# The squares of a decoder's first RMS norm, summed by TensorE alone, with its input loaded from two DMA queues

## The chip, the cores and the metric

The kernel runs on one core of a Trainium2 chip. The metric is the device time of one execution in microseconds (us). The core has five engines with instruction queues of their own: PE (TensorE: matrix products and transposes, with its weight loads listed as PEld), DVE (VectorE), ACT (ScalarE), POOL (GpSimd) and SP (SyncE, which issues DMAs here). Each engine works through its queue in order. An instruction whose input isn't ready holds up what is behind it on its own engine, and nothing else.

## The reference: what is computed

One inference step of a two-layer decoder, for a prompt of 512 tokens behind 16 meta tokens and for 8 sequences of 8 new tokens: 592 tokens of width 1024. Each layer is a gated feed-forward block, a mixer (a state-space scan and stick-breaking attention side by side, with a paged cache of keys and values for the new tokens) and a second feed-forward block, each behind an RMS norm. The change touches only the first norm, ahead of the first product:

```
def rms_norm(x, g):
    xf = x.astype(jnp.float32)
    y = xf * lax.rsqrt(jnp.mean(xf * xf, axis=-1, keepdims=True) + EPS)
    return (y * g.astype(jnp.float32)).astype(x.dtype)

def swiglu(h, w_gu, w_down):
    g, u = jnp.split(h @ w_gu, 2, axis=-1)
    return (jax.nn.silu(g) * u) @ w_down

x = x + 0.5 * swiglu(rms_norm(x, lp['norm_ffn1']), lp['ffn1_w_gu'], lp['ffn1_w_down'])
```

## The kernel before

All 592 tokens are processed at once, with the features on the partitions: x is eight tiles of 128 features by 592 tokens (`X[0]` to `X[7]`, k = 0 to 7). Products are kept close to float32 precision by splitting each operand into a high and a low part of a faster type and adding three products, high by high, high by low and low by high (`mm3`, L605, 128x128 by 128x296, two halves of the tokens). The weights come in blocks of 512 x 256 (`raw`, L586, three buffers) and are split half a block at a time: ACT makes the high part `whi` (L595), DVE the low part `wlo` (L596). A norm isn't applied ahead of its product: the product is made with the unscaled x times the gain, and its result is multiplied by R, the reciprocal root of each token's mean square, when it is evicted from PSUM (`times_r`, L231).

The first norm is built in `load_x`, called by `setup`. x is loaded from memory token by token, in six pieces (meta tokens, four blocks of 128 prompt tokens, 64 new tokens) and two halves of the features, all from SP's queue (L399), the first weight block between the halves. For each k, PE transposes the six pieces into two PSUM tiles `xps` (L406), DVE copies the first (L407) and ACT the second (L408) into `X[k]`. `norm_tile` then makes four things from `X[k]`: `xh`, the high part of x times the gain (L446, ACT); `xl`, the low part (L447, DVE); and the square `sq`, on GpSimd for even k (L451) or ACT for odd k (L453). The squares of k = 1 to 6 are added into that of k = 0 (L459), by GpSimd for k = 1, 3, 5 and by DVE for k = 2, 4, 6. `norm_end` hands the two remaining tiles to `factor`, a generator that runs a step with each product: it waits 8 steps, sums both tiles over the partitions with 10 one-column products on PE (L476, five groups of 128 tokens, two tiles), takes the reciprocal root on DVE (L522 to L529, some 14 instructions on five columns, one behind the other), waits 20 steps, spreads the result over the partitions with 10 products on PE (L208) and copies R from PSUM with ACT (L573). In the profile, a product on plain float32 operands such as L476 has two records. Until R is there (`hold`) the finished column blocks of the first product stay in PSUM; three fit, and the fourth has to wait for the first eviction.

The order of the instructions on each engine isn't written by hand. A scheduler places them by priority and by its own estimate of when each could run. In the mixers the program adds two small tables (`PRI` and `UNIT`) that set priorities of work that is to fill PE's gaps. An instruction that is placed elsewhere in the first norm can therefore change the order in a mixer 450 us later, though no line of it has changed. The feed-forward blocks have one chain of products, and leave the scheduler little to choose.

## Time and profile before

| | us |
|---|---|
| median of 3 runs | 2719.44 (2717.28 to 2721.03) |
| profiled execution, its own time | 2716.29 |
| its span in the trace | 2714.5 |
| PE busy | 2611.9 |
| DVE, ACT, GpSimd busy | 1505.0, 981.8, 315.6 |
| first norm, start to steady products | 50 |
| mixer 1, mixer 2 (first sum of the norm ahead to first sum of the norm behind) | 479.88, 483.83 |

All numbers of one row of a profile come from one execution. A row of the timeline gives the start, the time to the end of the last of its instructions, the engine, the line, the operation, output and inputs with their shapes, and how often it is repeated; in brackets stands the idle time of that engine ahead of it, and what ended it. A row of the waits says who waited for whom: total us, times, longest. In a row of the windows the busy time of each engine in one stretch is followed by the clock that TensorE was granted (1.00 is full speed), the share of the DMA engines' time in use, and the rate. A matrix instruction is recorded longer than it keeps the next from starting, so the spacing of starts is the price of one.

### The profile page before, as it was taken

The page shows a single profiled execution, that of the slowest core. Times are in us where ns is not written, and L with a number is a line of the kernel's source. Part 1 is how long each engine was busy: PE and PEld are TensorE (multiplying, and loading weights), DVE is VectorE, ACT ScalarE, POOL GpSimd, SP SyncE. Part 2 cuts the span into 40 slices and gives each one's busy share as a digit, 9 for nine tenths or more (in the row PEclk, how much of TensorE's full clock was granted, in tenths as well). Part 3 has the DMA queues.
Part 4 walks back from the last instruction along what each step waited for, and adds up shares of the span by engine and source line. Part 5 has one row for each costly group of instructions (what it writes and reads, how often), then busy time and mean ns, then how long its engine had stood idle before and what let it go on. Part 6 is the DMA issues. An engine that isn't in the chain of part 4 may idle for free.

```text
span 2714.5 us, 51301 instructions
## 1 busy us (share of the span) xinstructions
PE 2611.9 (96%) x21547; PEld 2469.2 (91%) x21547; DVE 1505.0 (55%) x3005; ACT 981.8 (36%) x1773; POOL 315.6 (12%) x288
## 2 busy tenths in 40 slices
PE   8999999999878999999999999999997899999999
PEld 7999999888656999999999999998875579999999
DVE  5444345477886744444554343454777867434444
ACT  3323224255654332222332222233556544323222
POOL 1000000024443100000000000000334431000000
PEclk9999999999998999999999999999998989999999
DMA  3232234347776122222222323254577762222222
GB/s 111 79 116 86 79 109 130 125 142 262 269 267 230 55 78 86 86 78 78 78 78 79 101 85 94 74 157 125 183 248 247 256 219 71 78 86 86 78 87 81
DMA packets 245111, 343.28 MB, mean 126 GB/s; under 512 B 32808, under 2 KB 196720, under 8 KB 244880
## 3 DMA queue, kind: packets, MB, share of 16 engines
q1 hardware_dynamic: 208016, 205.77, 24.5%
q0 software_dynamic: 36864, 134.23, 14.5%
q8 instruction: 169, 2.77, 0.4%
q14 instruction: 62, 0.51, 0.1%
HBM read 320.29 MB, written 19.66 MB: 125 GB/s over the span
## 4 chain that ended last, share of the span: by engine, by line
PE 60%; DVE 6%; DMA 3%; ACT 2%; issue 1%; POOL 0%; SPq 0%; DVEq 0%; ACTq 0%; POOLq 0%
PE g L605 53%; DVE kt L1493 2%; DMA v<-in_cache_v,vi 1%; PE v L926 1%; DMA kn<-in_cache_k,ki 1%; PE po L208 1%; PE po L211 1%; DVE st L1298 1%; DVE x L799 0%; PE pw L476 0%; PE z L211 0%; PE sc L211 0%; DVE pst L1298 0%; PE zt L1350 0%; PE pw L1534 0%
## 5 line engine op out<-in xcount | busy, mean ns | idle before, releaser
L605 PE MATMUL g<-xl,whi 128*128 128x296 f32 (+1 forms) x3392 | 1016.9, 300 | 1.7 <-DVE xl L447 1.7
L605 PE MATMUL g<-xh,wlo 128*128 128x296 f32 (+1 forms) x3392 | 1012.5, 299 | 3.4 <-DVE wlo L596 3.4
L605 PE MATMUL g<-xh,whi 128*128 128x296 f32 (+1 forms) x3392 | 1013.8, 300 | 1.6 <-DVE gs L231 1.2
L595 ACT ACTIVATE whi<-raw 128x512 fp32r<-128x512 f32 (+1 forms) x664 | 412.7, 622 | 1363.5 <-PE g L605 1280.4
L596 DVE TENSOR_TENSOR wlo<-raw,whi 128x512 fp32r<-128x512 f32 (+1 forms) x664 | 450.7, 679 | 598.0 <-ACT whi L595 541.1
L605 PEld LDWEIGHTS g<-xh,wlo 128*128 128x128 f32 x3392 | 640.2, 189 | 5.4 <-DVE wlo L596 4.1
L605 PEld LDWEIGHTS g<-xh,whi 128*128 128x128 f32 x3392 | 639.6, 189 | 6.0 <-issue 2.6
L605 PEld LDWEIGHTS g<-xl,whi 128*128 128x128 f32 x3392 | 640.6, 189 | 4.8 <-DVE xl L447 2.8
L605 PE MATMUL g<-hl,whi 128*128 128x296 f32 (+1 forms) x1408 | 417.9, 297 | 0.0
L605 PE MATMUL g<-hh,wlo 128*128 128x296 f32 (+1 forms) x1408 | 417.7, 298 | 0.0
L605 PE MATMUL g<-hh,whi 128*128 128x296 f32 (+1 forms) x1408 | 416.8, 298 | 0.0
L1487 POOL DMA_INDIRECT kn<-in_cache_k,ki x128 | 137.0, 1070 | 1554.6 <-PE g L605 931.5
L605 PEld LDWEIGHTS g<-hl,whi 128*128 128x128 f32 x1408 | 265.2, 188 | 0.0
L605 PEld LDWEIGHTS g<-hh,wlo 128*128 128x128 f32 x1408 | 264.3, 188 | 0.0
L605 PEld LDWEIGHTS g<-hh,whi 128*128 128x128 f32 x1408 | 263.9, 188 | 0.0
L1493 DVE STREAM_TRANSPOSE kt<-kn 128x512 f32<-128x512 f32 x256 | 163.4, 680 | 41.8 <-PE sc L211 21.7
L1552 POOL DMA_INDIRECT v<-in_cache_v,vi x128 | 144.2, 1127 | 280.6 <-DVE kt L1493 128.0
L704 DVE SCALAR_TENSOR_TENSOR x<-g,x 128x296 f32<-128x296 f32 (+1 forms) x192 | 88.2, 464 | 119.1 <-PE g L605 118.5
L231 DVE TENSOR_TENSOR us<-g,R 128x296 f32<-128x296 f32 (+1 forms) x176 | 81.6, 464 | 129.5 <-PE g L605 129.4
L231 DVE TENSOR_TENSOR gs<-g,R 128x296 f32<-128x296 f32 (+1 forms) x176 | 80.7, 464 | 123.1 <-PE g L605 121.4
L691 ACT ACTIVATE hh<-us 128x592 fp32r<-128x592 f32 (+1 forms) x88 | 61.2, 696 | 62.4 <-DVE us L689 62.4
L605 PE MATMUL g<-mh,whi 128*128 128x296 f32 (+1 forms) x256 | 78.0, 305 | 2.0 <-DVE ot L231 2.0
(372 smaller groups left out, 2894.5 us busy)
## 6 DMA issues: line engine op xcount, KB each, us to landing
raw<-in_ffn_w_gu SPq DMA_DIRECT2D x176, 512.0 KB
raw<-in_ffn_w_down SPq DMA_DIRECT2D x80, 512.0 KB
raw<-in_w_in SPq DMA_DIRECT2D x44, 512.0 KB
raw<-in_w_out SPq DMA_DIRECT2D x16, 512.0 KB
spill<-x SPq DMA_DIRECT2D x16, 296.0 KB
x<-spill SPq DMA_DIRECT2D x16, 296.0 KB
raw<-in_ffn_w_down SPq DMA_DIRECT2D x16, 256.0 KB
xt<-in_x_prompt SPq DMA_DIRECT2D x8, 256.0 KB
```

Source lines behind the costliest of these rows:

```text
L208: i = self.nc.tensor.matmul(*a, **k).ins
L211: i = self.nc.tensor.matmul(*a, **k).ins
L231: self.nc.vector.tensor_tensor(tv[0:P, h, :], ps[h][0:P, 0:self.n], rv[0:P, h, :], ALU.mult)
L595: nc.scalar.activation(hi[:, 0:nk], s, AF.Copy)
L596: nc.vector.tensor_tensor(lo[:, 0:nk], s, hi[:, 0:nk].bitcast(F32), ALU.subtract)
L605: mm = nc.tensor.matmul(ps[h][:, 0:self.n], w[:, k, :], self.hv(x)[:, h, :], start=(first and k == 0 and i == 0), stop=(last and k == nk - ...
L691: nc.scalar.activation(hh[:, a:b], u[:, a:b], AF.Copy)
L704: nc.vector.scalar_tensor_tensor(v, p, 0.5, v, ALU.mult, ALU.add)
L926: nc.tensor.matmul(ps[c], x[:, t0:t0 + 128], w.rearrange("p x c -> p (x c)"), start=(k == 0 and i == 0), stop=(k == 7 and i == 2))
L1487: nc.gpsimd.indirect_dma_start(kn, None, self.kflat, bass.IndirectOffsetOnAxis(ap=self.kidx[l][:, s, i:i + 1], axis=0))
L1493: nc.vector.transpose(kt[:, 2 * u:2 * u + 2].rearrange("p t h i -> p t (h i)"), kns[u][:, :, 256 * quad:256 * quad + 256])
L1552: nc.gpsimd.indirect_dma_start(v.rearrange("p k c -> p (k c)"), None, self.vflat, bass.IndirectOffsetOnAxis(ap=self.vidx[l][:, i, e:e + 1] ...
```

## The change

Four edits go together. All eight squares are made by ACT. None is added to another: for each k, PE sums the square at once with five one-column products that accumulate over k in one PSUM tile `B0`, 40 products in place of 10. `factor` then starts from these sums, without a wait of 8 steps. And every second piece of x (the first and third block of the prompt, and the new tokens) is issued from ACT's DMA queue; the meta tokens and the other two blocks stay on SP's.

```
         for h in range(2):
-            for (t, n, _), (s, _, _) in zip(toks, src):
-                nc.sync.dma_start(t[0:n, 512 * h:512 * h + 512], s[:, 512 * h:512 * h + 512])
+            for i, ((t, n, _), (s, _, _)) in enumerate(zip(toks, src)):
+                (nc.scalar if i % 2 else nc.sync).dma_start(t[0:n, 512 * h:512 * h + 512], s[:, 512 * h:512 * h + 512])
             if h == 0:
                 self.raw0 = self.raw(I["ffn1_w_gu"][0], 0, 4, 0, 256)
+        self.B0 = self.own("pw", [128, 128])
         for k in range(KD):
...
             if k == 0:
                 self.split0 = self.split(self.raw0, 4, 0)
-            self.norm_tile(k, "norm_ffn1", 0, nc.gpsimd if k in (1, 3, 5) else nc.vector,
-                           None if k % 2 else nc.gpsimd)
+            self.norm_tile(k, "norm_ffn1", 0, own=True)
+
+            for i, t0 in enumerate(self.groups()):
+                nc.tensor.matmul(self.B0[:, i:i + 1], self.sq[:, t0:t0 + 128], self.c_ones, start=(k == 0 and i == 0),
+                                 stop=(k == KD - 1), skip_group_check=True)
...
-    def norm_tile(self, k, nm, l, eng=None, sqeng=None):
+    def norm_tile(self, k, nm, l, eng=None, own=False):
...
         sq = self.tmp("sq")
-        if sqeng:
-            sqeng.tensor_tensor(sq[:, a:b], x[:, a:b], x[:, a:b], ALU.mult)
-        else:
-            nc.scalar.activation(sq[:, a:b], x[:, a:b], AF.Square)
-        if k == 0:
+        nc.scalar.activation(sq[:, a:b], x[:, a:b], AF.Square)
+        if own:
+            self.sq = sq
+        elif k == 0:
             self.acc = sq
...
-    def factor(self, squares, inv, wait):
+    def factor(self, squares, inv, wait, made=None):
...
-            A, B = self.own("po", [128, 512]), self.own("pw", [128, 128])
+            A, B = self.own("po", [128, 512]), made or self.own("pw", [128, 128])
...
     def norm_end(self):
-        self.factor([self.acc, self.sq], 1.0 / D, (8, 0, 20))
-        self.acc = self.sq = None
+        if self.B0:
+            self.factor([], 1.0 / D, (0, 0, 20), self.B0)
+        else:
+            self.factor([self.acc, self.sq], 1.0 / D, (8, 0, 20))
+        self.acc = self.sq = self.B0 = None
```

Lines of the changed kernel have moved by up to six: L605 is L611 there, L447 is L451, and the new sums are L415. Where the instructions now stand is shown at three places. The first is PE in the first norm, where the transposes of the second half of x begin (`xps`, the number tells one PSUM tile from the next). Before:

```order
L406 MATMUL xps_187<-call,xt 128x64
L406 MATMUL xps_203<-call,xt 128x16
L406 MATMUL xps_220<-call,xt 128x16
L406 MATMUL xps_237<-call,xt 128x16
L406 MATMUL xps_203<-call,xt 128x128
L406 MATMUL xps_220<-call,xt 128x128
L406 MATMUL xps_237<-call,xt 128x128
```

With the change, the same place, down to the first product of the feed-forward block (`g`):

```order
L407 MATMUL xps_263<-call,xt 128x128
L415 MATMUL pw<-call,sq 128x1 x10
L407 MATMUL xps_221<-call,xt 128x128 x2
L407 MATMUL xps_242<-call,xt 128x128 x2
L415 MATMUL pw<-call,sq 128x1 x10
L407 MATMUL xps_222<-call,xt 128x128
L407 MATMUL xps_222<-call,xt 128x64
L407 MATMUL xps_284<-call,xt 128x16
L407 MATMUL xps_284<-call,xt 128x128 x3
L611 MATMUL g_307<-xh,whi 128x296
```

The sums of the first four squares stand behind 30 and 34 of the 48 transposes, so that 20 sums, beside 46 transposes, now precede the first product. The other 20 sums follow after 18 products, with 31 products between them and the spread of R; before, the 10 sums came after 102 products.

The second place is ACT's queue from the start of the kernel. Before:

```order
L408 ACT_TABLE_LOAD
L408 ACTIVATE x_104<-xps_133 128x192
L408 ACTIVATE x_105<-xps_153 128x192
L408 ACTIVATE x_106<-xps_170 128x192
L446 ACTIVATE xh<-x_104,par 128x592
L453 ACTIVATE sq<-x_105 128x592
L595 ACTIVATE whi<-raw 128x512
```

With the change:

```order
L399 DMA xt<-in_x_prompt 128x512 x2
L399 DMA xt<-in_x_sample 64x512
L399 DMA xt<-in_x_prompt 128x512 x2
L399 DMA xt<-in_x_sample 64x512
L409 ACT_TABLE_LOAD
L409 ACTIVATE x_104<-xps_134 128x192
L450 ACTIVATE xh<-x_104,par 128x592
L454 ACTIVATE sq<-x_104 128x592
L454 ACTIVATE sq<-x_105 128x592
L601 ACTIVATE whi<-raw 128x512
L454 ACTIVATE sq<-x_106 128x592
```

Six DMA issues now precede the table load, and a square more stands ahead of the first `whi`. The last four issues each wait for an earlier transfer that used the same semaphore, the last two for blocks of the first half of x.

The third place is PE near the end of mixer 1, where the products with the gathered values (`po<-v,wt`) end and the output projection (`g<-mh,whi`) goes on. Before:

```order
L208 MATMUL po<-v,wt 32x256
L211 MATMUL po<-v,wt 32x256 x7
L208 MATMUL z_9608<-wp,vk 64x16
L211 MATMUL z_9608<-wp,vk 64x16 x15
L211 MATMUL z_9608<-w_9633,vk 64x16 x4
L208 MATMUL po<-v,wt 32x256
L211 MATMUL po<-v,wt 32x256 x7
L208 MATMUL po<-v,wt 32x256
L211 MATMUL po<-v,wt 32x256 x7
L208 MATMUL po<-v,wt 32x256
L211 MATMUL po<-v,wt 32x256 x7
L605 MATMUL g_9852<-mh,whi 128x296
```

With the change:

```order
L208 MATMUL po<-v,wt 32x256
L211 MATMUL po<-v,wt 32x256 x7
L208 MATMUL z_9583<-wp,vk 64x16
L211 MATMUL z_9583<-wp,vk 64x16 x15
L211 MATMUL z_9583<-w_9608,vk 64x16 x4
L1381 LDWEIGHTS mall
L1381 MATMUL z_9632<-mall 128x32
L1575 MATMUL po<-call,ob 128x16 x2
L611 MATMUL g_9845<-mh,whi 128x296
```

Three groups of such products have moved ahead of the `z` products, and the last step of that row of sequences (`po<-call,ob`) no longer has a projection product ahead of it. Counted instruction by instruction, with the numbers of the buffers left out, 646 of the 3197 PE instructions of mixer 1 stand elsewhere, and 316 of mixer 2; the two mixers of the kernel before differ from each other in 427. Outside the first norm and the mixers PE's order is as it was.

GpSimd loses its seven instructions of the first norm. The one that prepares its adds stood ahead of its first square and now stands ahead of its first add at the end of mixer 1, behind the last gather of that mixer.

## The prediction

> **What bounds the kernel now.** I read the page first, then the busy time by stretch of time, then the first 50 us instruction by instruction, then the waits. The first line says that PE is the engine to watch; the others, from the windows view, cut the run into the first norm (four rows), one piece of steady feed-forward work, a whole feed-forward stage and the two mixers. Their columns: length, busy us (records) of PE, PEld, DVE, ACT, POOL, then the granted clock, the DMA share and GB/s.
>
> ```profile
> PE 2611.9 (96%) x21547; PEld 2469.2 (91%) x21547; DVE 1505.0 (55%) x3005; ACT 981.8 (36%) x1773; POOL 315.6 (12%) x288
> 0.00:4.39 4.39, 0.31 (x1) 0.18 (x2) 0.48 (x3) 1.28 (x1) 1.94 (x13) 1.00 0.15 37
> 4.39:17.87 13.48, 10.05 (x47) 7.25 (x47) 7.26 (x11) 6.97 (x17) 4.63 (x4) 1.00 1.00 306
> 17.87:46.14 28.27, 24.76 (x180) 23.33 (x177) 21.21 (x56) 9.11 (x19) 5.86 (x4) 1.00 0.28 77
> 46.14:50.09 3.95, 3.95 (x18) 3.95 (x18) 2.58 (x6) 2.91 (x4) 0.00 (x0) 0.57 0.00 0
> 50.00:100.00 50.00, 50.00 (x369) 50.00 (x368) 22.46 (x37) 14.64 (x23) 0.00 (x0) 1.00 0.25 77
> 461.33:941.21 479.88, 436.61 (x4390) 369.76 (x4388) 345.36 (x785) 235.22 (x483) 140.77 (x126) 0.96 0.58 193
> 941.21:1369.94 428.73, 428.73 (x3145) 428.53 (x3144) 199.42 (x345) 126.27 (x199) 0.00 (x0) 1.00 0.26 81
> 1805.97:2289.80 483.83, 441.31 (x4390) 370.97 (x4388) 342.45 (x783) 240.36 (x485) 147.10 (x127) 0.95 0.58 193
> ```
>
> In the feed-forward stage PE has no idle time at all (428.73 of 428.73), and one product of 128x296 costs 50.00/369 = 0.1355 us. PE's order there is unchanged, so these stages neither gain nor lose. Only two places can move: the first norm, and the mixers, where PE idles 43.3 and 42.5 us and where the order of the instructions changes.
>
> In the first norm DMA is idle to begin with (share 0.15 until 4.39), then full until 17.87. After that DVE holds PE: it is busy in 21.21 of 28.27 us, with GpSimd beside it. These rows carry the durations (start, us, engine, line):
>
> ```profile
> 0.74 1.28 ACT L408 ACT_TABLE_LOAD   x1 [0.74 <-PEq L1619]
> 3.04 1.85 SPq L399 DMA_DIRECT2D xt<-in_x_prompt  x4
> 4.93 0.58 SPq L399 DMA_DIRECT2D xt<-in_x_sample  x1
> 8.98 7.26 PE L406 MATMUL xps<-call,xt 128*128 128x128 f32 x33 [0.95 <-DMA xt<-in_x_prompt]
> 10.90 0.78 ACT L408 ACTIVATE x<-xps 128x192 f32<-128x192 f32 x3 [8.88 <-PE xps L406]
> 11.31 2.31 POOL L451 TENSOR_TENSOR sq<-x 128x592 f32<-128x592 f32 x2 [8.84 <-ACT x L408]
> 11.55 0.80 ACT L446 ACTIVATE xh<-x,par 128x592 fp32r<-128x592 f32 x1
> 12.23 0.71 ACT L453 ACTIVATE sq<-x 128x592 f32<-128x592 f32 x1
> 12.65 1.60 DVE L447 SCALAR_TENSOR_TENSOR xl<-x,par,xh 128x592 fp32r<-128x592 f32 x1
> 12.82 0.64 ACT L595 ACTIVATE whi<-raw 128x512 fp32r<-128x512 f32 x1
> 13.34 0.34 ACT L408 ACTIVATE x<-xps 128x192 f32<-128x192 f32 x1
> 14.17 1.93 DVE L596 TENSOR_TENSOR wlo<-raw,whi 128x512 fp32r<-128x512 f32 x1
> 18.22 1.07 DVE L459 TENSOR_TENSOR sq<-sq 128x592 f32<-128x592 f32 x1
> 19.21 3.69 DVE L447 SCALAR_TENSOR_TENSOR xl<-x,par,xh 128x592 fp32r<-128x592 f32 x2
> 31.81 0.83 DVE L447 SCALAR_TENSOR_TENSOR xl<-x,par,xh 128x592 fp32r<-128x592 f32 x1
> 35.70 2.29 PE L476 MATMUL pw<-call,sq 128*128 128x1 f32 x20
> 37.85 0.38 PE L605 MATMUL g<-xl,whi 128*128 128x296 f32 x1
> 38.02 0.17 DVE L522 TENSOR_SCALAR rv<-pw 128x5 f32<-128x5 f32 x1 [1.11 <-PE pw L476]
> 40.48 0.17 DVE L529 TENSOR_TENSOR rlo<-ry,rhi 128x5 fp32r<-128x5 f32 x1
> 43.51 0.22 PE L208 MATMUL po<-identr,rhi 128*128 128x128 f32 x1
> 44.57 0.35 PE L605 MATMUL g<-xh,wlo 128*128 128x296 f32 x1
> 46.14 0.40 PE L605 MATMUL g<-xh,whi 128*128 128x296 f32 x1 [1.22 <-DVE gs L231]
> 50.09 0.30 PE L605 MATMUL g<-xh,wlo 128*128 128x296 f32 x1
> ```
>
> Two things are to be seen. While GpSimd squares and adds, DVE's own instructions stretch: an xl takes 1.60 or 1.85 us where the last one takes 0.83. So the last xl comes at 31.81, and the scale R only after that, so that PE waits 1.22 us for the first evicted block, at 46.14. Then PE runs at half speed until 50.09, when it settles.
>
> **The bookkeeping of the first norm, before.** From the first transpose at 4.39 to 50.09 are 45.70 us. In them PE does 48 transposes at 0.22 (33 in 7.26), 10.6 us. The three column blocks that precede 46.14 are 144 products (2 halves, 8 k, 3 terms each), and 17 more follow: 161 at 0.1355, 21.8 us. The 10 sums of squares take 2.15 (35.70 to 37.85), the 10 spreads of R 1.06 (43.51 to 44.57). That is 35.6 us of work; the other 10.1 us are 1.65 of half speed (3.95 minus 17 x 0.1355) and some 8.5 of waits.
>
> **The change, part by part.**
>
> *Sums.* 40 one-column products stand in place of 10. At 0.215 each (2.15/10) that adds 6.45 us to PE, which has no idle time later in the stage that could take them. The floor is thus 35.6 + 6.45 = 42.05 us with no wait at all: 46.45 in place of 50.09, a gain of 3.65. The other end keeps all 10.1 us of waits: a loss of 6.45. Those are the bounds of this stage.
>
> *DVE and GpSimd.* DVE loses three adds, the first 1.07; GpSimd loses all seven instructions here. With GpSimd silent the stretching goes: 0.77 on the first xl, 2.0 on the pair at 19.21, at least 1.1 on the wlo at 14.17 (1.93, against 0.83 for an xl, which is wider). So DVE's last xl, which then only follows its xh on ACT, should come before 25 in place of 31.81.
>
> *ACT* gets four more squares, at 0.59 start to start (12.23 to 12.82), 2.4 us, plus six DMA issues ahead of its table load. From its first copy, eight copies at 0.26, eight xh at 0.68, eight squares at 0.59 and three whi at 0.52 are 13.8 us. The issues cost 0.46 each (1.85/4), 2.8 us, and the last ones wait for first-half blocks to land; the cover is ACT's idle time until 10.90. If the copies could start by 8.1, table load and issues must be over by then: 0.74 + 2.8 + 1.28 = 4.8 leaves 3.3 us for those waits.
>
> *Loads.* ACT issues two of the four blocks of x at 0.74, not 3.04 and later; SP's two move up behind them, and the first weight block moves up past three issues, 1.4 us. The DMA share of 0.15 until 4.39 is room for the 1.18 MB of the first half (3.9 us at 306 GB/s). I take the copies to start at 8.1 instead of 10.90, with the 18 transposes ahead of them back to back from 4.39 (18 x 0.22 = 4.0).
>
> Here a rule of the Trainium skill speaks against the change: "DMA: Bandwidth & Descriptors", section "Issuing engines are not separate DMA queues", says that queues of several engines end on the same 16 DMA engines and that issuing from more saves only the issue time. From 4.39 to 17.87 the trace agrees (share 1.00 with one queue); until 4.39 it leaves room. By the rule alone x comes no earlier, which is the first rival below.
>
> *Does PE then wait?* In the new order PE meets the first sums after 30 transposes, at 4.39 + 6.6 = 11.0. ACT has that square at 8.1 + 0.78 + 0.68 + 0.59 = 10.15, the next at 10.74, the third (behind a whi) at 11.85, the fourth at 13.4, when PE needs them at 11.0, 12.1, 14.0 and 15.0. The last square is done at about 22 to 23; PE reaches it at about 25. The DVE chain from the sums to the low part of the factor (38.02 to 40.65, 2.6 us, with one wlo now between) fits under the 30 products (4.1 us) that stand before the spread. So nothing but the arrival of x is late, and I put the waits that remain at 1.6 us, of 0 to 4: the stage gains 3.65 - 1.6 = 2.0 us. It is near the floor because each engine in the walk is ahead of PE. The half speed after 46.14 I take as gone with the wait in front of it; if it returns, the gain is 0.4.
>
> On that stretch the skill's "TensorE: Matmul & The Clock Gate", section "What's actually happening", says that PE's default is half rate and a busy window of about 3.4 us releases it. By that rule the waits among sums and transposes could put the products that follow at half speed again, near 1.7 us; the row 4.39:17.87 shows a clock of 1.00 through as many waits, so I keep it out of the sum.
>
> *GpSimd's first add* moves to the end of mixer 1, with the set-up row ahead of it that stood before the first square; 51.5 us of idle time cover it, and the cost is nothing (without that cover, at most the 8.84 us that POOL idled here):
>
> ```profile
> 918.82 2.12 POOL L459 TENSOR_TENSOR sq<-sq 128x592 f32<-128x592 f32 x1 [51.52 <-issue]
> ```
>
> *The mixers.* The edit doesn't touch them, but 646 of PE's 3197 rows of mixer 1, and 316 of mixer 2, stand elsewhere. No row of before prices that. The nearest measure is before itself: its two mixers differ in 427 rows and take 479.88 and 483.83 us, although the second has 576 products of 288 columns in place of 296, 2.1 us less work. So two orders were 3.95 + 2.1 = 6.05 us apart. Grown with the root of the rows moved, that is 7.4 for mixer 1 and 5.2 for mixer 2, 9.1 together, of either sign; the middle is 0.
>
> **Sum.** Span 2714.5 - 2.0 = 2712.5; with the 1.8 us that lie around it (2716.29 was timed) 2714.3. The median of the runs is 3.15 above the profiled execution, so I forecast 2717.4. About 0.2% (5.4 us) is what a measurement of this kernel can tell from no change.
>
> **Rivals.**
>
> 1. *x comes no earlier*: DMA is full for 13 us anyway, and ACT's issues wait for landings. For it: the share of 1.00. Against: the empty start. The copies start at 10.7, 2.6 us later: 2717.4 + 2.6 = 2720.0. Chance 0.11, no change.
> 2. *The mixers' new order makes PE wait longer*, which is the slower side. Its place is the products of the values gathered from the cache, where the two orders of before already differ by 5.4 us:
>
> ```profile
> PE po L208 <- DMA v<-in_cache_v,vi: 15.8, 12, 3.0
> PE po L208 <- DMA v<-in_cache_v,vi: 10.4, 8, 2.2
> ```
>
> (mixer 1, then mixer 2). At 9.1 us lost the time is 2726.5. It decides once both mixers lose over 7.4. Against it: nothing in the edit pushes that way. With a spread of 9.1 the chance is 0.21; I give 0.18 of it here.
> 3. *PE waits for squares*: PE takes its rows in order, and the sums now stand among the transposes. It decides if over 9.0 us of waits stay; at the bound, 2719.4 + 6.45 = 2725.9. Chance 0.03.
> 4. *The mixers' order turns out shorter* by over 3.4: at 9.1, 2708.3. Chance 0.35, larger than rival 2 since the 2.0 us come on top.
>
> My forecast, both mixers together within -3.4 and +7.4 and the first norm as walked, has 0.33; with rival 1 that makes 0.44 for no change, 0.35 faster, 0.21 slower. The range is 2717.4 with 1.28 x 9.1 = 11.7 on either side, 2706 to 2729; the bounds of the first norm lie within it. The likeliest case's own range, with rival 1, is 2714 to 2725.
>
> **What would show it.** Right: the first ACT copy near 8.1; an xl at 0.83 throughout and the last before 25; 40 sums at 0.215; the product that stood at 50.09 (the 162nd) near 48; feed-forward stages of the same length to 0.5 us. Wrong: PE idle before L415 rows; the first copy after 10; a half-speed stretch after the sums. If the time moves by more than 5.4 us, the lengths of the two mixers must show it; if they don't and it does, this reading is wrong.

## The result, and the profile after

The changed kernel takes 2749.75 us (median of 6 runs, 2743.49 to 2759.51) against 2717.20 for the kernel before in the same session: a ratio of 1.0121, with a 95% interval of 1.0101 to 1.0141. It is slower by 1.2%, far outside the range of the prediction. Its profiled execution took 2749.72 us, with a span of 2747.9 against 2714.5.

The first question is where the 33.4 us lie. The first sum of squares of each norm (`pw<-call,sq`) marks the stages, so these first records cut the run. Columns: shortest, median and longest duration in ns, then the first and the last start in us.

```profile
L479 PE MATMUL pw<-call,sq x20: 164/250/250, 469.7 to 475.1; 128*128 128x1 f32 x20
L479 PE MATMUL pw<-call,sq x20: 166/250/250, 964.4 to 967.9; 128*128 128x1 f32 x20
L479 PE MATMUL pw<-call,sq x20: 164/250/250, 1393.7 to 1399.2; 128*128 128x1 f32 x20
L479 PE MATMUL pw<-call,sq x20: 164/250/250, 1829.4 to 1834.9; 128*128 128x1 f32 x20
L479 PE MATMUL pw<-call,sq x20: 164/250/250, 2324.9 to 2328.4; 128*128 128x1 f32 x20
```

The differences of these starts, to within 0.1 us, beside the same differences of every other run of this document (the labels are explained below):

| us | first norm and first stage | mixer 1 | stage | stage | mixer 2 | last stage | span |
|---|---|---|---|---|---|---|---|
| before | 461.3 | 479.9 | 428.7 | 436.1 | 483.8 | 424.7 | 2714.5 |
| changed | 469.7 | 494.7 | 429.3 | 435.7 | 495.5 | 423.0 | 2747.9 |
| e1 loads alone | 460.3 | 480.2 | 428.7 | 436.0 | 486.8 | 424.2 | 2716.2 |
| e2 sums alone | 471.2 | 476.5 | 427.6 | 435.1 | 489.1 | 423.3 | 2722.8 |
| e3 changed, old order of the mixers | 472.3 | 478.0 | 429.2 | 435.7 | 487.9 | 424.4 | 2727.5 |
| e4 before, new order of the mixers | 460.2 | 500.9 | 427.3 | 436.0 | 490.5 | 426.6 | 2741.5 |
| e5 five sums | 454.3 | 480.5 | 430.3 | 436.0 | 489.7 | 424.1 | 2714.9 |
| e6 sums among products | 479.3 | 478.1 | 428.6 | 436.0 | 488.0 | 423.9 | 2733.9 |
| e7 weights after x | 472.5 | 478.5 | 427.7 | 435.7 | 489.0 | 424.5 | 2727.9 |
| e8 wide sums | 466.5 | 480.4 | 427.6 | 435.7 | 489.2 | 424.1 | 2723.5 |
| e9 late blocks | 467.4 | 496.4 | 428.4 | 436.0 | 510.4 | 424.0 | 2762.6 |
| e10 warm start | 462.0 | 500.8 | 427.6 | 435.7 | 508.5 | 424.7 | 2759.3 |
| e11 ones matrix | 452.9 | 495.0 | 429.3 | 435.7 | 511.5 | 424.2 | 2748.6 |
| e12 ones matrix, two queues | 458.0 | 482.8 | 430.4 | 436.3 | 484.9 | 425.9 | 2718.3 |

Of the 33.4 us, 8.4 are in the first norm, 14.8 in mixer 1 and 11.7 in mixer 2; the feed-forward stages are as long as before, within 1.7. (e1 to e4, e5 to e8 and e12 ran on three chips on which the kernel before takes 2720 to 2722 us. e9 to e11 ran on another, where it takes 2764.5 and the mixers are longer in the old order too, so their mixers aren't compared with the rows above. Ratios are always within one chip. How well a stage repeats: e4 has the first norm of the kernel before, 460.2 and 461.3, and e3 that of the changed kernel, 472.3 and 469.7. With one profile of each, a difference of under 3 us in the first column says nothing.)

The windows view of the changed kernel, with the prediction's columns, for the first norm in two pieces and the two mixers:

```profile
5.43:27.94 22.51, 18.99 (x88) 16.38 (x87) 11.98 (x37) 11.61 (x24) 0.00 (x0) 0.66 0.60 175
27.94:58.40 30.46, 30.46 (x215) 30.21 (x214) 12.90 (x33) 12.11 (x20) 0.00 (x0) 0.91 0.18 53
469.69:964.39 494.70, 446.69 (x4389) 375.05 (x4388) 345.98 (x785) 236.01 (x483) 142.37 (x126) 0.95 0.56 187
1829.40:2324.92 495.52, 444.07 (x4389) 374.18 (x4388) 343.33 (x783) 240.29 (x485) 145.30 (x127) 0.94 0.57 188
```

In the first norm the granted clock is 0.66 and then 0.91, where it read 1.00 until the last 4 us (what that reading is worth is seen in e7). The mixers hold the same work: in mixer 1 the same records take 10.1 us longer (446.69 against 436.61 busy) and PE idles 4.7 us more; in mixer 2 it is 2.8 and 8.9.

The first norm, instruction by instruction (start, duration in us, engine, line):

```profile
5.43 3.41 PE L407 MATMUL xps<-call,xt 16*128 16x16 f32 x15
9.07 1.47 PE L407 MATMUL xps<-call,xt 64*128 64x64 f32 x9 [0.23 <-DMA xt<-in_x_sample]
9.47 0.78 ACT L409 ACTIVATE x<-xps 128x192 f32<-128x192 f32 x3 [1.73 <-PE xps L407]
13.83 1.90 PE L407 MATMUL xps<-call,xt 16*128 16x16 f32 x6 [3.29 <-DMA xt<-in_meta_tokens]
15.53 4.26 PE L415 MATMUL pw<-call,sq 128*128 128x1 f32 x20
20.54 4.27 PE L415 MATMUL pw<-call,sq 128*128 128x1 f32 x20
27.94 0.59 PE L611 MATMUL g<-xh,whi 128*128 128x296 f32 x1
31.85 4.52 PE L415 MATMUL pw<-call,sq 128*128 128x1 f32 x40
36.72 0.45 PE L611 MATMUL g<-xh,whi 128*128 128x296 f32 x1
39.68 0.45 PE L611 MATMUL g<-xh,whi 128*128 128x296 f32 x1
```

A sum is two records. The first 40 records come 0.21 us apart (4.26 for 20), the last 40 at 0.11 (4.52 for 40): from start to start the same sum costs 0.41 us or 0.22. A product of the first stretch takes 0.45 and comes 0.247 after the last, where 0.30 and 0.1355 are usual. PE thus ran at half speed until 29.9, with one break from 9.4 to 12.8 (there a transpose of 128x128 takes 0.27 in place of 0.42), and again from 36.7 to 40.1. DVE and GpSimd are no longer in the way: GpSimd does nothing here after its memsets, and every xl takes 0.83 or 0.84. Nevertheless the last xl starts at 32.23, no earlier than before (31.81), since it now waits for ACT, which waits for transposes.

### The profile page after: what moved, and what is told of

Same layout as the page of the kernel before. It is cut to its first block, busy times and chain, and to the rows that moved or that the text cites. A ratio compares the mean times of both kernels' runs of the same rounds, so it can differ in the third digit from the quotient of the medians.

```text
span 2747.9 us, 51383 instructions
## 1 busy us (share of the span) xinstructions
PE 2634.6 (96%) x21607; PEld 2489.0 (91%) x21607; DVE 1499.7 (55%) x3002; ACT 985.5 (36%) x1777; POOL 304.9 (11%) x281
## 4 chain that ended last, share of the span: by engine, by line
PE 83%; DVE 8%; DMA 4%; ACT 2%; issue 2%; POOL 0%; SPq 0%; DVEq 0%; POOLq 0%; ACTq 0%
PE g L611 72%; DMA v<-in_cache_v,vi 3%; DVE kt L1499 2%; PE v L932 2%; DMA kn<-in_cache_k,ki 1%; DVE st L1304 1%; PE po L208 1%; PE sc L211 1%; PE po L211 1%; PE pw L479 0%; PE pw L415 0%; POOL v L1558 0%; PE z L211 0%; DVE pst L1304 0%; DMA xt<-in_meta_tokens 0%
## 5 line engine op out<-in xcount | busy, mean ns | idle before, releaser
L611 PE MATMUL g<-xh,wlo 128*128 128x296 f32 (+1 forms) x3392 | 1014.5, 300 | 2.8 <-DVE wlo L602 2.8
L611 PE MATMUL g<-xl,whi 128*128 128x296 f32 (+1 forms) x3392 | 1016.6, 300 | 0.0
L611 PE MATMUL g<-xh,whi 128*128 128x296 f32 (+1 forms) x3392 | 1015.3, 300 | 0.1
L611 PEld LDWEIGHTS g<-xh,wlo 128*128 128x128 f32 x3392 | 641.3, 189 | 4.7 <-DVE wlo L602 3.3
L611 PEld LDWEIGHTS g<-xh,whi 128*128 128x128 f32 x3392 | 641.2, 189 | 3.4 <-issue 1.3
L611 PEld LDWEIGHTS g<-xl,whi 128*128 128x128 f32 x3392 | 641.7, 189 | 1.8 <-issue 1.3
L611 PE MATMUL g<-hl,whi 128*128 128x296 f32 (+1 forms) x1408 | 418.3, 298 | 0.0
L611 PE MATMUL g<-hh,wlo 128*128 128x296 f32 (+1 forms) x1408 | 417.3, 298 | 0.0
L611 PE MATMUL g<-hh,whi 128*128 128x296 f32 (+1 forms) x1408 | 416.2, 297 | 0.0
L611 PEld LDWEIGHTS g<-hl,whi 128*128 128x128 f32 x1408 | 265.0, 188 | 0.0
L611 PEld LDWEIGHTS g<-hh,wlo 128*128 128x128 f32 x1408 | 264.3, 188 | 0.0
L611 PEld LDWEIGHTS g<-hh,whi 128*128 128x128 f32 x1408 | 264.1, 188 | 0.0
L611 PE MATMUL g<-mh,whi 128*128 128x296 f32 (+1 forms) x256 | 78.4, 311 | 1.2 <-DVE ot L231 1.2
```

What stands on the lines that cost most here:

```text
L611: mm = nc.tensor.matmul(ps[h][:, 0:self.n], w[:, k, :], self.hv(x)[:, h, :], start=(first and k == 0 and i == 0), stop=(last and k == nk - ...
```

## The experiments

The theory at this point: 8.4 us come from the first norm, 26.5 from the order of the mixers, in which no line was changed. The rival: the mixers are slow because of what the first norm leaves behind it.

**e3 and e4: the order of the mixers alone.** At the end of the build, each engine's instructions of both mixers get an ordering dependency (no semaphore) on the one ahead in a written list of numbers. The list is that of the other kernel's order: the old order for e3, the new one for e4.

```diff
+        for s in d:
+            at += s
+            i = made[f"I-{at}"]
+            if last is not None:
+                self.tc.add_manual_dep(i, last.name, order, reason="pin")
+            last = i
```

> The changed kernel whole, but with every engine's instructions of the two mixers held in the order in which the kernel before issues them (no row of a mixer stands elsewhere than in the kernel before; the first norm is that of the changed kernel). Theory: the order alone lengthens the mixers, so they fall back to 480 and 484 us, within 1.5 each; the first norm stays 8.4 us longer; total 2723 to 2727. Rival A (the head's state slows the mixers): they stay at 494 and 495, total near 2750.

> The opposite: the kernel before whole, with every engine's instructions of the two mixers held in the order in which the changed kernel issues them; its first norm is untouched. Theory: start to first mixer 461.3 as before, mixers near 494.7 and 495.5 (within 2 each), total 2741 to 2746. Rival A: mixers near 480 and 484, total 2717.

e3 took 2725.48 us, a ratio of 1.0018 (1.0004 to 1.0032) to the kernel before; e4 took 2749.10, a ratio of 1.0112 (1.0094 to 1.0131). The mixers of e3, then those of e4, in the windows view:

```profile
472.30:950.30 478.00, 439.58 (x4390) 372.56 (x4389) 345.20 (x785) 235.58 (x483) 142.81 (x126) 0.96 0.58 194
1815.20:2303.10 487.90, 440.69 (x4389) 369.85 (x4388) 342.70 (x783) 240.31 (x485) 145.62 (x127) 0.95 0.57 191
```

```profile
460.20:961.10 500.90, 451.55 (x4389) 377.85 (x4388) 345.60 (x785) 236.06 (x483) 142.97 (x126) 0.94 0.56 185
1824.40:2314.90 490.50, 441.77 (x4390) 371.38 (x4389) 343.46 (x783) 240.30 (x485) 142.08 (x127) 0.95 0.57 190
```

The theory holds and the rival falls: the kernel before, given nothing but the new order, is as slow as the changed one, and the changed kernel with the old order loses all but 5 us of its loss. Going by the ratios, the order costs 30 us (0.0112 x 2720, of 26 to 36) and the rest of the change 5 (0.0018 x 2720, of 1 to 9; the profiles put it at 8 to 11). Their sum of 35 agrees, within these intervals, with the 33 of both. The split between the mixers is less sure. Mixer 1 took 478.0 to 482.8 us in the eight profiles with the old order (e9 to e11 left out), and 494.7 and 500.9 with the new one. Mixer 2 took 483.8 to 489.7 with the old and 495.5 and 490.5 with the new: the profile of before happened to have the shortest, and the order is worth some 5 us there.

What is different inside shows in the waits of PE (total us, times, longest). Mixer 1 before, then changed; mixer 2 changed:

```profile
PE po L208 <- DMA v<-in_cache_v,vi: 15.8, 12, 3.0
PE sc L208 <- DVE kt L1493: 2.8, 5, 1.1
```

```profile
PE po L208 <- DMA v<-in_cache_v,vi: 16.4, 14, 2.7
PE sc L208 <- DVE kt L1499: 5.4, 4, 3.4
PE zt L1356 <- DVE be L1349: 4.2, 3, 3.2
PE po L1575 <- DVE ob L1571: 2.2, 2, 1.8
```

```profile
PE po L208 <- DMA v<-in_cache_v,vi: 19.2, 11, 4.6
```

In mixer 2 the gathers, which were waited for 10.4 us, are waited for 19.2: here the prediction had named the right place. In mixer 1 they are as before, and several short waits on DVE and ACT have grown instead: `be` from 1.2 to 4.2 and `ob` from nothing to 2.2. The longest on `ob` is at 842.55, behind `zt` products; at the third place shown ahead of the prediction, where `po<-call,ob` no longer has a projection product ahead of it (903.9), PE doesn't wait. The two swaps bear this out: with the new order, e4 waits 5.0, 4.2 and 2.4 for `kt`, `be` and `ob` in mixer 1 and 16.3 for the gathers in mixer 2; with the old one, e3 has 2.8, 1.2, nothing and 11.4. The rest of the loss is busy time at a lower clock (10 of the 15 us of mixer 1). The trace's record of the clock has PE at half speed for 34.1 us of mixer 1 before and 41.0 in e3, but 51.2 in the changed kernel and 61.4 in e4; in mixer 2 it is 58.0 in the changed kernel and 51.2 in the other three. That the longer waits bring this on is likely, but no run took the two apart.

**e1: the loads alone.** The kernel before with this one line; the scheduler moved nothing in the mixers.

```diff
-            for (t, n, _), (s, _, _) in zip(toks, src):
-                nc.sync.dma_start(t[0:n, 512 * h:512 * h + 512], s[:, 512 * h:512 * h + 512])
+            for i, ((t, n, _), (s, _, _)) in enumerate(zip(toks, src)):
+                (nc.scalar if i % 2 else nc.sync).dma_start(t[0:n, 512 * h:512 * h + 512], s[:, 512 * h:512 * h + 512])
```

> The kernel before with one part of the change alone: x comes from two queues; squares, adds and sums stay as before. No instruction of either mixer moves against the kernel before (0 rows on any engine). Theory (the 33 us are two things: 8.4 us in the first norm, from x pieces that land late when two queues and raw0 share the DMA, with TensorE idle and then at half clock; 26.5 us in the mixers, from their new order): mixers stay at 480 and 484 us, the first norm grows by 2 to 5 us over 461.3, total 2717 to 2722. Rival A (the mixers are slow because of what the head leaves behind, the second queue above all): mixers near 494, total near 2743. Rival B (the loads do help by 1 to 3 us, and the sums cost everything that the first norm lost): start to first mixer 458 to 460, total 2714 to 2716.

2719.79 us, a ratio of 1.0002 (0.9991 to 1.0013). The first norm took 460.3 us, between the 460.2 and 461.3 of two profiles without the change. The theory (2 to 5 us lost by late pieces of x) falls, and so does the gain of rival B: the two queues do nothing. Two rows show why:

```profile
10.28 0.78 ACT L408 ACTIVATE x<-xps 128x192 f32<-128x192 f32 x3 [2.06 <-PE xps L406]
13.86 6.14 PE L406 MATMUL xps<-call,xt 16*128 16x16 f32 x22 [1.85 <-DMA xt<-in_meta_tokens]
```

The first copy comes only 0.6 us earlier than before, and PE then waits 1.85 us for the second half of the meta tokens, asked for behind the first weights (0.2 before; in e7, which asks for the weights last, the wait is gone). PE also starts later: its first instruction waits 5.2 to 5.7 us for the rows of the gains (`prow`) in every run with two queues, and 3.8 to 4.0 with one (e10, which starts with products, left out).

**e2: the sums alone.** The changed kernel with the old lines of loads.

```diff
-            for i, ((t, n, _), (s, _, _)) in enumerate(zip(toks, src)):
-                (nc.scalar if i % 2 else nc.sync).dma_start(...)
+            for (t, n, _), (s, _, _) in zip(toks, src):
+                nc.sync.dma_start(...)
```

> The changed kernel with the loads on one queue again: squares by ScalarE, 40 sums in place of 10 and no adds. Against the kernel before 62 PE rows of the first mixer and 436 of the second stand elsewhere (the changed kernel: 820 and 349). Theory: with x on one queue TensorE doesn't wait for meta tokens until 13.8 us; the first norm is 3 to 6.5 us longer than before (the 30 extra sums), against 8.4; the first mixer, with few rows moved, is within 4 us of 480, the second 8 to 15 us longer than 484; total 2730 to 2740. Rival A (head's state, not order, slows the mixers): both mixers are alike, either both near 494 (sums are the cause) or both near 480 (loads are). Rival B (sums alone cost the head's loss): the first norm 8 us longer or more.

2727.59 us, a ratio of 1.0034 (1.0022 to 1.0045). The first norm took 471.2 us, 9.9 more than before and no less than with the two queues, so it is rival B's second half that holds: the sums cost all that the first norm lost. The mixers, of which 62 and 436 rows had moved (820 and 349 with the change, by the same count), took 476.5 and 489.1: this draw of the order cost nothing that can be seen.

```profile
13.30 2.13 PE L415 MATMUL pw<-call,sq 128*128 128x1 f32 x10
30.32 6.63 PE L415 MATMUL pw<-call,sq 128*128 128x1 f32 x40
42.38 0.42 PE L611 MATMUL g<-xh,wlo 128*128 128x296 f32 x1
```

From 13.30 on PE never waits, and yet the records of sums are 0.21 us apart, the products that follow run at half speed until 29.0, and the block at 30.32 falls from 0.11 to 0.21 within itself and leaves half speed behind until 42.6. So the new question was what makes PE run at half speed.

**e5: five sums.** From here on the mixers are held in the old order.

```diff
             for i, t0 in enumerate(self.groups()):
-                nc.tensor.matmul(self.B0[:, i:i + 1], ...
+                if k == 0:
+                    nc.tensor.matmul(self.B0[:, i:i + 1], ...
```

> The changed kernel with x on one queue, and only the 5 sums of the first tile of x left; the other 35 are left out, so R comes from an eighth of the squares. The mixers are held in the order of the kernel before. Theory now: it is the blocks of one-column sums that bring TensorE to half speed in the first norm, after which they, the transposes and the products beside them all take twice as long. Then without them transposes stay near 0.22 us, the first products come 0.135 us apart, and start to first mixer is 452 to 456 us (461.3 less the 8.5 us of waits for squares and less 1 us of sums, give or take 2); total 2707 to 2713. Rival C (half speed comes from the empty stretches and the transposes before the first product, whatever the sums do): the first products come 0.245 us apart until about 29 us, first norm 457 to 460.

2714.53 us, a ratio of 0.9972 (0.9962 to 0.9983), and a first norm of 454.3: 7.0 less than before. That is about what the old sums, adds and their waits cost (this kernel leaves out 35 of the 40 sums). Two rows of PE:

```profile
18.61 0.59 PE L612 MATMUL g<-xh,whi 128*128 128x296 f32 x1
20.16 0.30 PE L612 MATMUL g<-xh,whi 128*128 128x296 f32 x1
```

Half speed was still there at the first products (until 20.0), so rival C is right that it doesn't begin with the sums, but without them it ends 9 us earlier than in e2.

**e7: no empty stretch.** The first piece of weights is asked for behind both halves of x.

```diff
-            if h == 0:
+            if h == 1:
                 self.raw0 = self.raw(I["ffn1_w_gu"][0], 0, 4, 0, 256)
```

> The changed kernel, sums in blocks and x on two queues, but the first piece of weights (raw0) is asked for after the second half of x instead of between the halves; mixers in the order of the kernel before. It takes away TensorE's wait of 3.29 us for the second half of the meta tokens. Theory: the blocks of sums halve the speed all the same, start to first mixer 465 to 470. Rival C (the empty stretch at 10.5 to 13.8 us halves it, the sums are innocent): speed stays full, sums at 0.107 us a record, first norm 457 to 461.

2730.41 us, a ratio of 1.0028 (1.0014 to 1.0041); first norm 472.5, 2.5 above what I expected. PE never waits from its first transpose on, and half speed lasts without a break until 42.4. The last row is of the windows view, over the block of sums:

```profile
5.82 8.85 PE L407 MATMUL xps<-call,xt 16*128 16x16 f32 x36
28.64 8.53 PE L415 MATMUL pw<-call,sq 128*128 128x1 f32 x40
42.11 0.45 PE L611 MATMUL g<-xh,whi 128*128 128x296 f32 x1
```

```profile
30.00:35.00 5.00, 5.00 (x25) 5.00 (x25) 0.00 (x0) 0.00 (x0) 0.00 (x0) 1.00 0.00 0
```

Rival C's empty stretch falls as the cause. And the granted clock stands at 1.00 in the middle of 40 records that come 0.21 us apart: this column doesn't always show half speed. The durations do. In each of the fourteen profiles the column reads 1.00 until the durations first change to full speed (here at 42.4), and in the first norm agrees with them from then on.

**e8: the same sums, 64 columns wide.**

```diff
-                nc.tensor.matmul(self.B0[:, i:i + 1], self.sq[:, t0:t0 + 128], self.c_ones, ...
+                nc.tensor.matmul(self.B0[:, i, :], self.sq[:, t0:t0 + 128], self.c_ones.to_broadcast([128, 64]), ...
```

> The kernel of the second run (40 sums in blocks, x on one queue), with one number changed: each sum writes 64 equal columns instead of one, so it streams 64 times as much and loads the same weights. Mixers in the order of the kernel before. Theory, in its sharper form (what halves the speed is that a one-column sum keeps the array empty): with 64 columns the speed stays full, a sum costs 0.2 to 0.3 us, first norm 458 to 465. Rival E (it is the weight loads, or the transposes between the blocks): speed halves as before, first norm 471 or more.

2722.40 us, a ratio of 0.9998 (0.9982 to 1.0014): no difference from the kernel before. The profile puts the first norm at 466.5, 4.7 less than e2's and between the two expectations (5.2 above before, where the interval of the ratio leaves 3.8 at most). The mixers are held, as they weren't in e2; in the first norm the columns are all that differs.

```profile
18.72 4.37 PE L415 MATMUL pw<-call,sq 128*128 128x64 f32 x20
30.29 4.57 PE L415 MATMUL pw<-call,sq 128*128 128x64 f32 x40
```

The early blocks run at half speed as in e2, but the block at 30.29 keeps 0.11 us a record to its end, and full speed after it, where e2's fell. A sum with more columns costs no more and didn't bring half speed on here, yet it doesn't end it.

**e6: a product behind each sum.** The squares wait in eight buffers, and an ordering dependency puts one product between any two sums.

```diff
+                    self.tc.add_manual_dep(mm, self.product.name, ..., reason="turn")
+                    self.turnmm = mm
...
+                    if self.turnmm:
+                        self.tc.add_manual_dep(mm, self.turnmm.name, ..., reason="turn")
```

> All 40 sums, x on one queue, no adds, but each sum put behind one product of the first projection (one sum, one product, and so on, from the 31st product), instead of in blocks of 10, 10, 20 and 40 records between the transposes; the squares stay in eight buffers until then. Mixers in the order of the kernel before. Theory: with products between them the sums don't halve the speed, each costs 0.215 us, 6.45 us more than the 10 of before, and the waits for squares are gone (8.5): start to first mixer 458 to 461.5, total 2713 to 2719, the gain that the prediction put at 2.0. Rival D (sums cost what they cost wherever they stand, and halve the speed there too): 467 or more, total over 2724.

2735.77 us, a ratio of 1.0042 (1.0028 to 1.0056); first norm 479.3, the longest. PE waited for three xl (2.7 us between 21.2 and 25.5), went to half speed, and stayed there for the whole of the 40 pairs and 11 products more, to 56.1:

```profile
25.50 0.62 PE L617 MATMUL g<-xl,whi 128*128 128x296 f32 x1 [0.67 <-DVE xl L450]
48.91 0.59 PE L617 MATMUL g<-xl,whi 128*128 128x296 f32 x1
```

The theory's remedy failed, in the direction of rival D: with one sum for each product PE is never idle and doesn't recover before the sums end. Here it was the waits ahead of the first sum that brought half speed on; the sums only kept it.

**e9: late blocks of ten.** PE's order in the first norm written as a list: 75 products, then four blocks of 10 sums with 14 products between.

```diff
+        for x, y in zip(HEAD, HEAD[1:]):
+            self.tc.add_manual_dep(made[f"I-{y}"], f"I-{x}", order, reason="head")
```

> All 40 sums again, x on one queue, squares kept in eight buffers, but PE's order in the first norm written out by hand: 75 products, 10 sums, 14 products, 10 sums, 14, 10, 14, 10, then 18 products and the spreads of R. Mixers in the order of the kernel before. Theory (TensorE starts every run at half speed, transposes of 0.421 us with weight loads of 0.222 are its sign, of 0.273 and 0.138 the sign of full speed; one-column sums in the half-speed stretch cost 0.425 and keep it at half; sums that come when it runs at full speed, 10 at a time, cost 0.215 as in the kernel before): full speed before the first block, 40 sums near 8.6 us, products 0.135 apart between the blocks; start to first mixer 459 to 464, total 2715 to 2721. Rival D (40 sums halve the speed wherever they stand): half speed from the second or third block on, first norm 467 or more.

2770.37 us against 2764.53 on this chip, a ratio of 1.0025 (1.0008 to 1.0042); first norm 467.4. The last two rows are of the windows view.

```profile
29.62 2.29 PE L479 MATMUL pw<-call,sq 128*128 128x1 f32 x20
37.90 2.29 PE L479 MATMUL pw<-call,sq 128*128 128x1 f32 x20
42.88 4.26 PE L479 MATMUL pw<-call,sq 128*128 128x1 f32 x20
```

```profile
37.57:40.98 3.41, 3.41 (x31) 3.41 (x30) 0.69 (x1) 0.09 (x1) 0.00 (x0) 1.00 0.41 120
40.98:51.22 10.24, 10.24 (x46) 10.24 (x46) 2.86 (x15) 0.63 (x1) 0.00 (x0) 0.50 0.12 30
```

The first three blocks (the second, at 33.77, isn't shown) cost 0.215 us a sum, the price of the kernel before; 1 us behind the third PE falls to half speed, and the fourth costs 0.41. So half of the theory stands (at full speed a sum costs 0.215, early ones are dear because PE is at half speed), and so does half of rival D (enough of them bring half speed on at any place).

How many are enough can be read from the traces. In the first norm of every run the clock changes only at instants that lie 3.41 us, or a whole multiple of it, apart (20.50, 40.98 and 51.22 here); where they lie differs from run to run. Cut into such stretches of 3.41 us, PE at full speed and never idle fell to half speed behind those that held 2.05 us of one-column sums or more (2.05 in e10, 2.09 in e2, 2.15 here at 37.57, 2.8 in e3, 2.9 in the changed kernel), and not behind those that held 2.04 or less (2.04 in e4, 1.84 in e1, 1.76 here at 34.16, 1.52 before); the limit is inferred from these nine stretches alone. It rose again only behind stretches that held less than 0.3 us of them; those of e6, with 1.1 to 1.5 us each, kept it down. A block of ten takes 2.15 us, so whether it costs half speed depends on whether it falls into one stretch: e9's third did, that of the kernel before was cut in two.

**e10: a warm start.** The kernel before, with 22 products of zeros ahead of all else.

```diff
+        for _ in range(22):
+            nc.tensor.matmul(wp[:, 0:296], wz[:, 0:128], wz[:, 0:296], start=True, stop=True)
```

> The kernel before with 22 products of zeros on TensorE ahead of everything, while it has nothing to do (their result is not used); nothing else differs, mixers in the order of the kernel before. Theory (half speed at the start is TensorE's own state, and work ends it): the 22 products run 0.247 us apart at first, and the transposes behind them already at full speed (0.273 us, weight loads 0.138, instead of 0.421 and 0.222). The first norm gains little, since x arrives until 13 us and VectorE's copies of x are next: 459 to 462, total 2714 to 2720. Rival F (0.421 is what a transpose costs): the transposes keep 0.421.

2761.15 us, a ratio of 0.9985 (0.9972 to 0.9998), at most a small gain, and none in the first norm: 462.0. The first two rows are the transposes of the kernel before, early and late; the last two those of e10, early and late (durations in ns: shortest, median, longest).

```profile
L406 PE MATMUL xps<-call,xt x21: 222/421/476, 11.7 to 16.0; 128*128 128x128 f32 x14, 64*128 64x64 f32 x4, 16*128 16x16 f32 x3
L406 PE MATMUL xps<-call,xt x4: 230/273/328, 17.4 to 17.8; 128*128 128x128 f32 x3, 16*128 16x16 f32 x1
```

```profile
L411 PE MATMUL xps<-call,xt x8: 208/272/327, 7.1 to 7.9; 128*128 128x128 f32 x6, 16*128 16x16 f32 x2
L411 PE MATMUL xps<-call,xt x13: 282/421/474, 14.1 to 17.4; 128*128 128x128 f32 x9, 64*128 64x64 f32 x3, 16*128 16x16 f32 x1
```

A transpose takes 0.421 us at half speed and 0.272 at full speed, so rival F falls: PE starts every run at half speed, the 22 products end that state (at 6.26), and it comes back at 13.1, behind 3.41 us of transposes alone. In the kernel before, too, all transposes until 15.8 ran at half speed, under a granted clock of 1.00. Full speed for the early ones didn't shorten the first norm, since x comes no faster.

Further on, one block of ten sums with products on both sides is enough to bring half speed on:

```profile
36.88 2.29 PE L481 MATMUL pw<-call,sq 128*128 128x1 f32 x20
40.51 0.45 PE L610 MATMUL g<-xh,whi 128*128 128x296 f32 x1
```

**e11 and e12: sums as wide products.** A matrix of ones is the weight, each rounded square streams past it, and R is worked out on 128x592.

```diff
+            for k, t in enumerate(squares):
+                for p, c, m in ((A, 0, 512), (B, 512, n - 512)):
+                    nc.tensor.matmul(p[:, 0:m], self.onesr, t[:, c:c + m], start=(k == 0), stop=(k == KD - 1))
```

> The sums made differently: a 128x128 matrix of ones as the weights, and each square (rounded to the reduced float32 that the products use) streamed past it, 512 and 80 columns, eight times, so that 16 instructions give the sum on every partition and the 40 one-column sums and 10 spreads are gone; R is then worked out by VectorE on 592 columns. x on one queue, mixers in the order of the kernel before. Theory: sums that stream many columns cost 0.3 us a tile, 2.4 in all, and count as work like products, so the half-speed stretch ends as it does without sums; start to first mixer 452 to 457 (454.3 with five sums), total 2708 to 2715, the one version that beats the kernel before. Rival G (R now needs about 10 VectorE instructions of 0.6 us in a row, while VectorE splits weights and x): R comes after 38 us and PE waits for free banks, first norm 458 to 464.

2752.10 us against 2764.53 on this chip, a ratio of 0.9960 (0.9944 to 0.9976): faster than both kernels, as expected; first norm 452.9.

```profile
13.88 0.78 PE L593 MATMUL po<-sq,onesr 128*128 128x512 f32 x1
18.00 0.48 PE L593 MATMUL po<-sq,onesr 128*128 128x512 f32 x1
18.57 0.30 PE L640 MATMUL g<-xl,whi 128*128 128x296 f32 x1
```

Half speed ends among these sums, at 16.6: one takes 0.78 us at 13.88 and 0.48 at 18.00, and the products already take 0.30 at 18.57. Half speed doesn't come back, though five more sums of this kind stand among the products. That the sums themselves end it isn't shown: in e12 half speed lasts past five of the eight. R is ready at 36.4, before PE needs a free bank, so rival G falls.

e12 is e11 with x on two queues, as in the change, and the weights asked for behind it, as in e7.

```diff
-                nc.sync.dma_start(t[0:n, 512 * h:512 * h + 512], s[:, 512 * h:512 * h + 512])
+                (nc.scalar if i % 2 else nc.sync).dma_start(t[0:n, 512 * h:512 * h + 512], s[:, 512 * h:512 * h + 512])
-            if h == 0:
+            if h == 1:
```

> The ones-matrix sums of the run before, with both halves of x from two queues and the first weights asked for behind x; mixers in the order of the kernel before. Theory: the early transposes lose their waits for x (2.5 us in the run before) but the first product waits for weights that land later; start to first mixer 450 to 454, ratio 0.995 to 0.998. Rival H (x from two queues brings nothing once weights come later): first norm 454 or more, ratio over 0.998.

2714.36 us against 2721.11, a ratio of 0.9974 (0.9964 to 0.9983); first norm 458.0. Still faster than both kernels. Rival H holds for the stage, 5 us longer than with one queue, but not for the ratio, which it put over 0.998: the first products come at 20.46 instead of 18.35, and PE is at half speed until 26.0 instead of 16.6. By the ratios e11 and e12 can't be told apart; by the first norm one queue with wide sums, and the old order of the mixers, is the better version.

## Why the prediction was wrong, point by point

Two terms of the sum failed. The mixers' new order, put at 0 with a spread of 9.1 us, lost 26.5 (points 7 and 8). The first norm, put at a gain of 2.0, lost 8.4 (points 2 to 6).

1. *Feed-forward stages unchanged:* right, within 0.6 us for the two in the middle; the last is 1.7 shorter (423.0, where the other runs have 423.3 to 426.6).
2. *DVE and GpSimd:* right in mechanism (every xl takes 0.83 or 0.84, GpSimd is silent, and its first add at the end of mixer 1 waits only for ACT's square), but "before 25" for the last xl was wrong (32.23). What held it was no longer DVE but ACT, and behind ACT the transposes.
3. *Loads:* the step "the copies start at 8.1" failed. They started at 9.47, and with the loads alone (e1) at 10.28. PE's first transpose came at 5.43, behind a longer wait for the rows of the gains, and it still had to wait for the last piece of the first half. Rival 1 was right: two queues bring nothing (1.0002). The rule that the prediction put beside it, from the Trainium skill's "DMA: Bandwidth & Descriptors", section "Issuing engines are not separate DMA queues", agrees with e1.
4. *40 sums at 0.215:* this term was mis-sized. It came from a row at 35.70, where PE runs at full speed, and was moved to 15 us, where it doesn't (0.41 a sum). Measured from start to start, the blocks of the changed kernel take 4.12, 4.12 and 4.38, 12.6 us instead of 8.6.
5. *"So nothing but the arrival of x is late", waits of 1.6 us, half speed gone:* failed. PE began 1.0 us later (5.43 against 4.39) and waited 0.23 and 3.29, so 4.6 us in place of 1.6; products at half speed cost 2.5 more (8 from 27.94 and 14 from 36.72, at 0.247 or less in place of 0.1355), transposes 0.55. With the 4.0 of the sums that is 10.1 us, of the 10.4 between the forecast (2.0 gained) and the result (8.4 lost). The product that was put near 48 (the 162nd) came at 58.41, after 50.09 before. The long wait alone explains little: e2 and e7 are without it, and their first norms are no shorter.
6. *The clock rule kept out of the sum:* this is the step behind 4 and 5. The Trainium skill's "TensorE: Matmul & The Clock Gate", section "What's actually happening", was weighed and set aside because the granted clock read 1.00 from 4.39 to 17.87. The durations of that very stretch said half speed: 0.22 us a transpose (7.26 for 33), which the prediction took as what a transpose costs; at full speed they come 0.11 apart. The trace agrees with the rule: in e10 22 products at the start end half speed, and the clock changes in steps of 3.41 us. The price given beside it, 1.7 us, was also too low, as it left out that the sums keep the state up: sums, products and transposes lost 7 us by half speed.
7. *The mixers:* the mechanism of rival 2 was right and its size wrong by three times. The spread of 9.1 us was scaled from the 6.05 us between the two mixers of before; the new order costs 26.5 in the two profiles, about 30 by e4's ratio. Its place was half right (mixer 2's gathers, +8.8 us; not mixer 1's). The count of moved rows, by whose root the spread was scaled, says little: e2 moved more rows of mixer 2 than the change did (436 to 349) and took 489.1 there, no more than other runs in the old order. Whether "the middle is 0" holds for an order that was tuned is open: of two draws, e2's changed nothing that can be told and the new one lost 1.1%.
8. *The test named in advance* (a change of over 5.4 us must show in the lengths of the mixers) came out: 26.5 of 33.4.

What stays open: how much of the mixers' loss is waiting and how much the lower clock, and how far transposes count as work for the clock. In the kernel before (at 15.8) and in the changed one (at 9.4) full speed came after transposes alone, in e7 36 transposes without a wait didn't bring it, and in e10 transposes lost it. The Trainium skill's "TensorE: Matmul & The Clock Gate", section "Part 4: PE-mode transpose", says that they don't count as work in the same way; e10 and e7 agree, the kernel before and the changed one do not.

## What to carry to other kernels

A schedule that a scheduler derives from a tuned table is part of the kernel: any edit ahead of it can reorder stages that the edit doesn't touch, so compare the orders first, and hold the old order (or tune again) before judging the edit. Price an instruction at the speed of the place that it moves to: take TensorE's speed from the durations of records there, not from the clock column or from a row elsewhere. Sums with one output column cost as much as sums with 64 and can put TensorE at half speed; the same sums as a matrix of ones with a wide moving operand cost less, and half speed didn't return behind them (e11, e12).

## What the runs showed of the hardware, unexpected

- One-column sums hold TensorE at half speed while it is never idle: 26.6 us of sum and product in turn in e6 (26.40 to 53.0). At full speed they bring half speed on once they fill 2.05 of the 3.41 us between two possible changes of the clock (e2, e3, e9, e10, changed kernel), and 2.04 us didn't (e4).
- The granted clock reads 1.00 ahead of its first change, though PE runs at half speed (e7, 30 to 35 us; before, until 15.8).
- The same order of instructions takes 478 to 490 us a mixer on one chip and 495 to 512 on another (e9 to e11; the kernel before, 2764.5 against 2717 to 2722).
